# Column sums of an 8192x8192 fp32 matrix: casts and bf16 matmuls replaced by a running sum on VectorE and fp32 matmuls in four column tiles

## The chip, the cores and the metric

The kernel runs on one core of a Trainium2 chip. The metric is the device time of the program in microseconds (us): the median of ten runs before the change, and one further execution taken by the hardware profiler, from which the views below come.

## The reference

```python
def setup_inputs():
    return {"x": np.random.randn(8192, 8192).astype(np.float32)}

def reference(x):
    return np.sum(x, axis=0)
```

The output is one row of 8192 fp32 sums, one for each column of x. The matrix has 268 MB, all of which must be read once; the output has 32 KB.

## The kernel before

The matrix is cut into 64 blocks of 128 rows. In a block each row lies on a partition of its own, and one load of 4 MiB, issued from SyncE's queue (SP, L46), brings the whole block (`xt`, 128x8192 fp32) into SBUF. `xt` has four buffers, so up to four loads are issued ahead; the load of block i+4 waits until both casting engines are done with block i.

Each block is cast to bf16 (`xb`, three buffers) in four strips of 2048 columns: strips 0 and 2 on ScalarE (ACT, L50), strips 1 and 3 on VectorE (DVE, L52). Then TensorE (PE) sums over the partitions: 16 matmuls per block (L60), each with a single column of 128 ones as the stationary operand and 512 columns of `xb` as the moving one. The result of a matmul is one row of 512 sums. The first eight column groups add into partition 0 of `psum`, the other eight into partition 64, at the group's offset; the accumulation runs over all 64 blocks (`start` at the first, `stop` at the last), so the running sum stays in PSUM until the end.

After the last block VectorE copies partition 0 of `psum` to SBUF (`res`, L69), ScalarE copies partition 64 (L70), and SP stores the two halves (L71, L72).

The order of the work is that of the program on each engine; the Tile framework puts in the waits between engines and for free buffers. No order is written out by hand.

Of the kernel before, what the change touches and what calls it, by code (L numbers as in the profile page):

```python
# [1 line left out]

# [4 lines left out]


@with_exitstack  # L10
def kernel(
    ctx: ExitStack,
    tc: tile.TileContext,
    x: bass.AP,
    out: bass.AP,
):
    nc = tc.nc
    P = nc.NUM_PARTITIONS
    R, C = x.shape
    assert R % P == 0  # L20
    n_row_blocks = R // P

    N = 512
    assert C % N == 0
    n_col_groups = C // N
    HALF = C // 2

    xr = x.rearrange("(b p) c -> b p c", p=P)

    const_pool = ctx.enter_context(tc.tile_pool(name="const", bufs=1))  # L30
    load_pool = ctx.enter_context(tc.tile_pool(name="loads", bufs=4))
    bf_pool = ctx.enter_context(tc.tile_pool(name="bf", bufs=3))
    psum_pool = ctx.enter_context(tc.tile_pool(name="psum", bufs=1, space=bass.MemoryType.PSUM))
    out_pool = ctx.enter_context(tc.tile_pool(name="out", bufs=1))

    ones = const_pool.tile([P, 1], mybir.dt.bfloat16)
    nc.gpsimd.memset(ones, 1.0)  # L37

    psum = psum_pool.tile([P, HALF], mybir.dt.float32)

    nsplit = 4
    CS = C // nsplit
    for i in range(n_row_blocks):
        xt = load_pool.tile([P, C], mybir.dt.float32)
        xb = bf_pool.tile([P, C], mybir.dt.bfloat16)
        nc.sync.dma_start(out=xt, in_=xr[i])  # L46
        for s in range(nsplit):
            eng = nc.scalar if s % 2 == 0 else nc.vector
            if eng is nc.scalar:
                eng.copy(out=xb[:, s * CS:(s + 1) * CS], in_=xt[:, s * CS:(s + 1) * CS])  # L50
            else:
                eng.tensor_copy(out=xb[:, s * CS:(s + 1) * CS], in_=xt[:, s * CS:(s + 1) * CS])  # L52
        for g in range(n_col_groups):
            if g < n_col_groups // 2:
                opart = 0
                off = g * N
            else:
                opart = 64
                off = (g - n_col_groups // 2) * N
            nc.tensor.matmul(  # L60
                out=psum[opart : opart + 1, off : off + N],
                lhsT=ones,
                rhs=xb[:, g * N : (g + 1) * N],
                start=(i == 0),
                stop=(i == n_row_blocks - 1),
            )

    res = out_pool.tile([P, HALF], mybir.dt.float32)
    nc.vector.tensor_copy(out=res[0:1, :], in_=psum[0:1, :])  # L69
    nc.scalar.copy(out=res[64:65, :], in_=psum[64:65, :])  # L70
    nc.sync.dma_start(out=out[0:HALF], in_=res[0:1, :])  # L71
    nc.sync.dma_start(out=out[HALF:C], in_=res[64:65, :])  # L72


# [1 line left out]
_INS = ['x']  # L76
_OUTS = [((8192,), 'float32')]


# [23 lines left out]
```

## Time and profile before

| | us |
|---|---|
| median of 10 runs | 646.08 |
| lowest to highest | 645.23 to 646.59 |
| profiled execution, its own time | 645.64 |
| span of the profiled execution, first to last instruction | 643.8 |
| TensorE matmuls busy (1024) | 337.7 |
| ScalarE busy (130) | 241.6 |
| VectorE busy (129) | 155.6 |
| mean DMA rate over the span | 417 GB/s |

The mean granted clock of TensorE was 0.707 of full speed. How the profile is read: the page's first part gives busy time per engine, with the number of instructions; its second part cuts the span into 40 slices and gives the busy share of each in tenths. The chain of waits follows the work that ended last back from the end: a line has its start, its length and what the time went to, either an instruction or the wait for a load. The timeline lists instructions with start, length, engine, line (L50 is line 50 of the kernel), operation, output and input, and in brackets how long the engine had been idle and what ended that. A group of instructions shows, after its shapes and count, the total busy time in us and the mean of one in ns, and then the idle time ahead of it. A busy TensorE is not TensorE at its peak: its matmuls are pipelined and their ends are modelled.

### The profile page before, as it was taken

What the parts mean: (1) busy time and instruction counts of PE and PEld (TensorE: products, weight loads), DVE (VectorE), ACT (ScalarE), POOL (GpSimd) and SP (SyncE); (2) the same over time, 40 slices, a digit from 0 to 9 for tenths busy, and PEclk for the clock granted to TensorE, in tenths of its full rate; (3) what the DMA queues carried; (4) which work ended last, traced back from release to release, by engine and by line L of the source; (5) the groups of instructions that cost most, each with busy time, mean ns of one, the idle gap of its engine ahead of it and who ended that gap; (6) DMA issues with size and microseconds to landing.
All of it is one profiled execution on the core that took longest, in us unless ns stands there. A gap on an engine that the chain in (4) does not pass through costs nothing.

```text
span 643.8 us, 2724 instructions
## 1 busy us (share of the span) xinstructions
PE 337.7 (52%) x1024; PEld 97.6 (15%) x1024; DVE 155.6 (24%) x129; ACT 241.6 (38%) x130; POOL 0.3 (0%) x5
## 2 busy tenths in 40 slices
PE   1464654645645644655546546645556447446542
PEld 0111111111111111111111111111111111111110
DVE  1122122221221221221221221221221222222213
ACT  2244242442442442442442432433433433423423
POOL 0000000000000000000000000000000000000000
PEclk9767668667677687677666766687677776776676
DMA  9999999999999999999999999999999999999980
GB/s 385 430 423 436 441 423 425 438 440 424 422 442 432 429 423 446 425 432 422 444 428 432 426 439 428 434 425 440 429 432 427 434 436 427 430 436 436 425 347 2
DMA packets 9233, 268.64 MB, mean 417 GB/s; under 512 B 1026, under 2 KB 1026, under 8 KB 1026
## 3 DMA queue, kind: packets, MB, share of 16 engines
q1 hardware_dynamic: 9220, 268.47, 97.0%
q8 instruction: 8, 0.13, 0.1%
q14 instruction: 5, 0.04, 0.0%
HBM read 268.44 MB, written 0.03 MB: 417 GB/s over the span
## 4 chain that ended last, share of the span: by engine, by line
DMA 88%; ACT 5%; issue 4%; DVE 1%; PE 1%; SPq 0%; ACTq 0%
DMA xt<-in_x_dram 88%; ACT xb L50 5%; DVE res L69 1%; PE psum L60 1%; ACT res L70 1%; SPq L46 0%; ACTq L50 0%
## 5 line engine op out<-in xcount | busy, mean ns | idle before, releaser
L60 PE MATMUL psum<-xb,ones 128*1 128x512 bf16 x1024 | 337.7, 572 | 295.4 <-DVE xb L52 289.5
L50 ACT CAST xb<-xt 128x2048 bf16<-128x2048 f32 x128 | 236.7, 1896 | 391.9 <-DMA xt<-in_x_dram 391.9
L52 DVE CAST xb<-xt 128x2048 bf16<-128x2048 f32 x128 | 151.2, 1224 | 478.1 <-DMA xt<-in_x_dram 478.1
L60 PEld LDWEIGHTS <-ones 128*1 128x1 bf16 x1024 | 97.6, 107 | 535.0 <-issue 522.2
L70 ACT COPY res<-psum 1x4096 f32<-1x4096 f32 x1 | 3.6, 3562 | 7.0 <-DVE res L69 7.0
L69 DVE COPY res<-psum 1x4096 f32<-1x4096 f32 x1 | 4.4, 4410 | 3.9 <-PE psum L60 3.9
L50 ACT ACT_TABLE_LOAD x1 | 1.3, 1283 | 0.7 <-PEq L87 0.7
L37 POOL MEMSET ones<- 128x1 bf16 x1 | 0.1, 102 | 0.3 <-POOLq L87 0.3
L87 POOL MEMSET const-bfloat16-1.0<- 128x1 bf16 x1 | 0.1, 101 | 0.0
L87 POOL MEMSET const-uint8-127<- 128x1 uint8 x1 | 0.1, 101 | 0.0
L87 POOL MEMSET const-float32-0.0<- 128x1 f32 x1 | 0.1, 98 | 0.2 <-issue 0.2
L87 POOL MEMSET const-float32-1.0<- 128x1 f32 x1 | 0.1, 98 | 0.0
## 6 DMA issues: line engine op xcount, KB each, us to landing
xt<-in_x_dram SPq DMA_DIRECT2D x64, 4096.0 KB, 35.0
out_dram<-res SPq DMA_DIRECT2D x2, 16.0 KB
```

Source lines behind the costliest of these rows:

```text
L37: nc.gpsimd.memset(ones, 1.0)
L50: eng.copy(out=xb[:, s * CS:(s + 1) * CS], in_=xt[:, s * CS:(s + 1) * CS])
L52: eng.tensor_copy(out=xb[:, s * CS:(s + 1) * CS], in_=xt[:, s * CS:(s + 1) * CS])
L60: nc.tensor.matmul(out=psum[opart : opart + 1, off : off + N], lhsT=ones, rhs=xb[:, g * N : (g + 1) * N], start=(i == 0), stop=(i == n_row ...
L69: nc.vector.tensor_copy(out=res[0:1, :], in_=psum[0:1, :])
L70: nc.scalar.copy(out=res[64:65, :], in_=psum[64:65, :])
L87: nc = _bacc.Bacc("TRN2", target_bir_lowering=False, num_devices=1)
```

## The change

- A load now brings two adjacent rows of x to each partition: 32 blocks of 256 rows, 8 MiB each (`xt`, 128 partitions x 2 rows x 8192 columns, 64 KB on each partition), in three buffers instead of four. There is no cast and no bf16 tile.
- For tiles 0 to 29 VectorE carries a running sum. In each tile it adds the running sum of the tile before (that tile's second row) to the first row, in place, and then the first row to the second row, in place; the second row is the running sum from there on. In tile 0 there is only the second of these adds.
- TensorE works only at the end. The stationary operand is 128x32 fp32 ones. The 8192 columns are cut into six pieces of 2048, 2048, 2048, 1024, 512 and 512 columns; each piece is cut into four parts, and part j is summed into the partitions 32j to 32j+31 of the piece's own PSUM tile (one of the four column tiles of the array). First come all pieces of tile 29's running sum, then both rows of tile 30 (`near`), then, piece by piece, both rows of tile 31 (`last`).
- Tile 30 is one load. Tile 31 is loaded in five strips of 4096, 2048, 1024, 512 and 512 columns, all from SP's queue.
- As soon as a piece has its last matmul, VectorE copies its PSUM tile to SBUF and four rows of it (partitions 0, 32, 64, 96) are stored: from SP's queue, for the last piece from ScalarE's.

```diff
+STRIPS = [
+    [(2048, 4), (2048, 4)],
+    [(2048, 4)],
+    [(1024, 4)],
+    [(512, 4)],
+    [(512, 4)],
+]
...
-    xr = x.rearrange("(b p) c -> b p c", p=P)
+    xr = x.rearrange("(b p k) c -> b p k c", p=P, k=K)
...
-    load_pool = ctx.enter_context(tc.tile_pool(name="loads", bufs=4))
-    bf_pool = ctx.enter_context(tc.tile_pool(name="bf", bufs=3))
...
+    load_pool = ctx.enter_context(tc.tile_pool(name="loads", bufs=3))
...
-    ones = const_pool.tile([P, 1], mybir.dt.bfloat16)
+    ones = const_pool.tile([P, 32], F32)
...
+    def column_sums(src, piece, start, stop):
+        _, c0, w, nj, n, ps, _ = piece
+        for j in range(nj):
             nc.tensor.matmul(
-                out=psum[opart : opart + 1, off : off + N],
+                out=ps[32 * j : 32 * j + 32, :],
                 lhsT=ones,
-                rhs=xb[:, g * N : (g + 1) * N],
-                start=(i == 0),
-                stop=(i == n_row_blocks - 1),
+                rhs=src[:, c0 + j * n : c0 + (j + 1) * n],
+                start=start,
+                stop=stop,
+                skip_group_check=True,
             )
...
+    prev = None
+    for t in range(n_blocks - 2):
+        xt = load_pool.tile([P, K, C], F32, tag="xt")
+        nc.sync.dma_start(out=xt, in_=xr[t])
+        a, b = xt[:, 0], xt[:, 1]
+        if prev is not None:
+            nc.vector.tensor_tensor(out=a, in0=a, in1=prev[:, 1], op=ADD)
+        nc.vector.tensor_tensor(out=b, in0=b, in1=a, op=ADD)
+        prev = xt
+
+    near = load_pool.tile([P, K, C], F32, tag="xt")
+    nc.sync.dma_start(out=near, in_=xr[n_blocks - 2])
+    last = load_pool.tile([P, K, C], F32, tag="xt")
+    t = n_blocks - 1
+    c = 0
+    for strip in STRIPS:
+        w = sum(w for w, _ in strip)
+        nc.sync.dma_start(out=last[:, :, c : c + w], in_=xr[t][:, :, c : c + w])
+        c += w
+
+    for piece in pieces:
+        column_sums(prev[:, 1], piece, True, False)
+    for piece in pieces:
+        for k in range(K):
+            column_sums(near[:, k], piece, False, False)
+    for piece in pieces:
+        s, c0, w, nj, n, ps, res = piece
+        for k in range(K):
+            column_sums(last[:, k], piece, False, k == K - 1)
+        rows = 32 * nj
+        nc.vector.tensor_copy(out=res[0:rows, :], in_=ps[0:rows, :])
+        eng = nc.scalar if s == len(STRIPS) - 1 else nc.sync
+        eng.dma_start(
+            out=out[c0 : c0 + w].rearrange("(j i) -> j i", j=nj),
+            in_=res[0 : 32 * (nj - 1) + 1 : 32, :],
+        )
```

More of the change, by code (lines that the diff above doesn't have):

```diff
@@ L7 @@
 from concourse._compat import with_exitstack
+F32 = mybir.dt.float32
+ADD = mybir.AluOpType.add
+STRIPS = [
[5 more added lines that the diff above has]
+]
 @with_exitstack
@@ L19 @@
     R, C = x.shape
[L20 to L26, printed above, removed]
-    xr = x.rearrange("(b p) c -> b p c", p=P)
-    const_pool = ctx.enter_context(tc.tile_pool(name="const", bufs=1))
-    load_pool = ctx.enter_context(tc.tile_pool(name="loads", bufs=4))
-    bf_pool = ctx.enter_context(tc.tile_pool(name="bf", bufs=3))
-    psum_pool = ctx.enter_context(tc.tile_pool(name="psum", bufs=1, space=bass.MemoryType.PSUM))
@@ L34 @@
-    out_pool = ctx.enter_context(tc.tile_pool(name="out", bufs=1))
-    ones = const_pool.tile([P, 1], mybir.dt.bfloat16)
-    nc.gpsimd.memset(ones, 1.0)
[L39 to L59, printed above, removed]
+    K = 2
@@ new lines @@
+    assert R % (P * K) == 0
+    assert sum(w for s in STRIPS for w, _ in s) == C
+    n_blocks = R // (P * K)
+    xr = x.rearrange("(b p k) c -> b p k c", p=P, k=K)
+    const_pool = ctx.enter_context(tc.tile_pool(name="const", bufs=1))
+    load_pool = ctx.enter_context(tc.tile_pool(name="loads", bufs=3))
+    psum_pool = ctx.enter_context(
+        tc.tile_pool(name="psum", bufs=1, space=bass.MemoryType.PSUM)
+    )
+    ones = const_pool.tile([P, 32], F32)
+    nc.gpsimd.memset(ones, 1.0)
@@ L60 @@
+    pieces = []
+    c0 = 0
+    for s, strip in enumerate(STRIPS):
+        for w, nj in strip:
+            n = w // nj
+            i = len(pieces)
+            ps = psum_pool.tile([P, n], F32, name=f"ps{i}", tag=f"ps{i}")
+            res = const_pool.tile([P, n], F32, name=f"res{i}", tag=f"res{i}")
+            pieces.append((s, c0, w, nj, n, ps, res))
+            c0 += w
+    def column_sums(src, piece, start, stop):
+        _, c0, w, nj, n, ps, _ = piece
+        for j in range(nj):
             nc.tensor.matmul(
-                out=psum[opart : opart + 1, off : off + N],
+                out=ps[32 * j : 32 * j + 32, :],
@@ L62 @@
                 lhsT=ones,
-                rhs=xb[:, g * N : (g + 1) * N],
-                start=(i == 0),
-                stop=(i == n_row_blocks - 1),
-            )
[L68 to L72, printed above, removed]
+                rhs=src[:, c0 + j * n : c0 + (j + 1) * n],
@@ new lines @@
+    nc.sync.dma_start(out=near, in_=xr[n_blocks - 2])
[21 more added lines that the diff above has]
+            in_=res[0 : 32 * (nj - 1) + 1 : 32, :],
+        )
```

## The prediction

> **What bounds the kernel now.** I read the page first: the span, the slices, the queue that carries the loads.
>
> ```profile
> span 643.8 us, 2724 instructions
> PE 337.7 (52%) x1024; PEld 97.6 (15%) x1024; DVE 155.6 (24%) x129; ACT 241.6 (38%) x130; POOL 0.3 (0%) x5
> DMA  9999999999999999999999999999999999999980
> q1 hardware_dynamic: 9220, 268.47, 97.0%
> ```
>
> No engine is busy for more than 52% of the span, while the load queue is busy for 97% of it. The DMA slices are full from the first to the 38th and drop only in the last two. So the span is a load stream with a short head and a tail that does no loading. The chain of waits gives the period of the stream and the pieces of the tail.
>
> ```profile
> 2.12 39.97 DMA xt<-in_x_dram
> ...
> 45.91 36.57 DMA xt<-in_x_dram
> ...
> 86.30 35.04 DMA xt<-in_x_dram
> ...
> 125.17 35.02 DMA xt<-in_x_dram
> ...
> 588.14 1.74 issue
> ...
> 591.80 35.01 DMA xt<-in_x_dram
> 626.90 1.91 ACT xb L50
> 628.85 4.32 PE psum L60 x15
> 633.20 4.42 DVE res L69
> 637.65 3.56 ACT res L70
> ```
>
> Each link of the chain is four loads deep, one turn of the four buffers. From 86.30 to 125.17 are 38.87 us, so one 4 MiB load takes 9.72 us, or about 432 GB/s (4.194 MB / 9.72 us). The tail begins where the last load has landed, at 626.90, and lasts 643.8 − 626.90 = 16.9 us: casts, matmuls, a copy on VectorE, a copy on ScalarE that waits for VectorE, a store. Nothing of it lies beside loading. The timeline gives the same landings directly, through the casts that wait for them, and the last store.
>
> ```profile
> 0.73 35.72 SPq L46 DMA_DIRECT2D xt<-in_x_dram  x7
> 12.97 3.70 ACT L50 CAST xb<-xt 128x2048 bf16<-128x2048 f32 x2 [10.96 <-DMA xt<-in_x_dram]
> 588.08 3.70 ACT L50 CAST xb<-xt 128x2048 bf16<-128x2048 f32 x2 [6.02 <-DMA xt<-in_x_dram]
> 607.50 3.70 ACT L50 CAST xb<-xt 128x2048 bf16<-128x2048 f32 x2 [6.01 <-DMA xt<-in_x_dram]
> 626.90 3.70 ACT L50 CAST xb<-xt 128x2048 bf16<-128x2048 f32 x2 [6.00 <-DMA xt<-in_x_dram]
> 641.23 0.25 SPq L72 DMA_DIRECT2D out_dram<-res  x1
> ```
>
> The profiled execution took 645.64 us, 1.84 us more than its span, and lies 0.07% under the median of 646.08. I work on its trace and add the 1.84 us at the end.
>
> **The stream.** The same 268 MB are loaded in the same order, in 8 MiB loads: one per two of the old. At 2 × 9.72 = 19.4 us each, tile 31 (the last) lands at 626.9, tile 30 at 607.5 and tile 29 at 588.1, the rows above. The first load is issued at 0.73 and lands at 12.97, so 12.24 − 9.72 = 2.5 us are lead-in, unchanged. Removing the casts takes nothing from this; they run beside the stream.
>
> Two things could move the stream. Half as many loads could lose less between loads, and the second link (45.91 to 86.30, 40.4 us) lost 1.5 us at the start that may not recur: a gain of at most about 2 us. The last tile comes as strips of 4096, 2048, 1024, 512 and 512 columns, so its rows arrive in shorter runs (2 KB in the end). If the two 512-column strips, 1 MiB or 2.4 us together, ran at half rate, that is 2.4 us more; no row shows it. I take +0.5 us, nearer to the full rate that all the loads show, which puts the last landing at 627.4.
>
> **VectorE's sum.** This is new and must fit beside the stream. Each of 30 tiles gets two fp32 adds of 128x8192 (the first tile one). The trace has no two-input operation; the nearest rows are these.
>
> ```profile
> L52 DVE CAST xb<-xt 128x2048 bf16<-128x2048 f32 x128 | 151.2, 1224 | 478.1 <-DMA xt<-in_x_dram 478.1
> L69 DVE COPY res<-psum 1x4096 f32<-1x4096 f32 x1 | 4.4, 4410 | 3.9 <-PE psum L60 3.9
> L60 PEld LDWEIGHTS <-ones 128*1 128x1 bf16 x1024 | 97.6, 107 | 535.0 <-issue 522.2
> ```
>
> By the cast an add takes 4 × 1.22 = 4.9 us, by the PSUM copy 2 × 4.41 = 8.8 us. An add reads two streams, so I take the slower row: 8.7 us, as its fixed part (some 0.14 us) comes once for 8192 columns, not twice. Two adds are 17.4 us against 19.4 us per tile: hidden, with a slack of 2 us per tile, and VectorE is never behind when a tile lands. The cover is gone when an add exceeds 9.7 us.
>
> The loads wait for VectorE now: tile t's buffer is free when the first add of tile t+1 has read its second row, 8.7 us after that tile landed. In the three-buffer rotation load t+2 is then still running for another 19.4 − 8.7 = 10.7 us, and the lead-in is 2.5 us, so SP's queue has the next load waiting in time. Behind a waiting load on SP stand only later loads and, at the very end, the stores. The strips of tile 31 wait for the first add of tile 29 (588.1 + 8.7 = 596.8), before tile 30 has landed.
>
> **TensorE at the end.** This decides the case. TensorE does nothing until tile 29's sum is complete at 588.1 + 17.4 = 605.5. Then it must take in one row per partition of that sum, two of tile 30 and two of tile 31: in units of one 128x512 fp32 matmul 16 + 32 + 32 = 80, in order. Call the price of one unit, after whatever the four column tiles gain by running side by side, p. The trace has only bf16 matmuls; these two windows cover one burst of 16, at half clock and then near full.
>
> ```profile
> 618.50:621.50 3.00, 2.93 (x9) 0.97 (x10) 1.10 (x1) 2.41 (x2) 0.00 (x0) 0.50 0.96 415
> 621.50:623.20 1.70, 1.70 (x10) 0.42 (x6) 0.00 (x0) 0.00 (x0) 0.00 (x0) 0.94 1.07 463
> ```
>
> The columns are length, busy time by engine, granted clock, DMA share, GB/s. In time at full clock the burst is 3.00 × 0.50 + 1.70 × 0.94 = 3.1 us for 16 matmuls, 0.19 us each; the first 3 us of a burst cost double, 1.5 us once.
>
> The ends for p: 0.05 us if an fp32 matmul costs a bf16 one's time and all four tiles gain fully (0.19 / 4), and 0.76 us if it costs double for its double bytes, double again because the clock stays at the 0.50 of the first window, and the tiles gain nothing (0.19 × 2 × 2). I take 0.19 us, the row as it stands: two effects of unknown size pull on it from opposite sides. [...]
>
> With p = 0.19: tile 29's sum takes 605.5 to 610.0, tile 30 until 616.1. Tile 31's strips land at about 617.2, 622.1, 624.5, 625.7 and 627.4 and need 16, 8, 4, 2 and 2 units, each done before the next lands: TensorE is idle when the last strip comes. What follows 627.4 is two units (0.4), VectorE's copy of 128 columns out of PSUM (4410 − 4096 / 0.96 = 143 ns fixed and 133 ns of columns: 0.3) and the store, 643.8 − 641.23 = 2.6 us from issue to the end as now, plus 0.1 us of handing on: 3.4 us. ScalarE's queue, which issues this store, holds nothing else. The other copies and stores fall while later strips are loading.
>
> Sum: 643.8 − 16.9 + 0.5 + 3.4 = 630.8 us of span, 632.6 us with the 1.84. Against 645.64 that is a gain of 13 us, 2.0%, all of it the tail.
>
> When p grows, the backlog does not matter up to 0.26 us, as TensorE still waits for the last strip. Beyond, TensorE runs without a pause from 605.5: the time is 605.5 + 1.5 + 80p + 2.95 (copy, store and handing on) + 1.84 = 611.8 + 80p. Ten nanoseconds of p are 0.8 us of the kernel, and the old time of 646.1 is reached at p = 0.43 us.
>
> **Rivals.** First: the column tiles run one after the other (which is also the case that the change does not do what it says, four tiles at once). With p = 0.76 the time is 611.8 + 60.8 = 672.6 us, 4% slower; the point from which this decides is p = 0.43 us. For it: in the trace matmuls follow one another strictly, and no two outputs in neighbouring column tiles are ever in work together, so no gain is shown. Against it: the four outputs of a group lie on separate partitions and depend on nothing of each other, and a price between these ends is enough.
>
> Second: the tiles overlap, but each matmul shows its weight load. That load takes 107 ns in the row of VectorE's fence, so p = 0.19 + 0.11 = 0.30 us, and the time 611.8 + 24 = 635.8 us; with a larger fp32 load or a weaker gain, up to p = 0.42 and 645 us. For it: 120 matmuls (6 pieces, 4 tiles, 5 rows) each load 32 columns of fp32 instead of one of bf16. Against it: in the two windows 16 loads (0.97 + 0.42 us busy) lie inside time in which TensorE is busy throughout (2.93 of 3.00, 1.70 of 1.70), so today they cost nothing. [...]
>
> Third: VectorE becomes the bound. Tile 0 lands 31 × 19.4 before 626.9, at about 25. At an add of 10.5 us, 59 adds end at 25 + 59 × 10.5 = 644.5, and all 80 units, the copy and the store follow: 1.5 + 15.2 + 2.95 + 1.84, together 666 us. It decides from 9.7 us. For it: an add reads two streams and writes one in place while the DMA fills the same memory; against it: no row of VectorE is slower than 1.08 ns per column (4410 / 4096), and 8192 of those are 8.8 us.
>
> Fourth: the stream gains its 2 us and the strips cost nothing: about 630 us.
>
> **How the numbers follow.** About 0.2% (1.3 us) is what a measurement of this kernel can tell from no change. The forecast (p up to 0.26, stream as now or slightly better) has 0.64, the fourth case 0.04 of its own, the second, between 635 and 645 us, 0.14; the first from p = 0.44 up has 0.11, VectorE or a slower stream 0.04. About 0.03 is left for a p close to 0.43, where the tail merely changes its owner. So faster 0.82, within 0.2% 0.03, slower 0.15. The predicted time is 632.6 us. The range is 629.5 to 645: the lower end is the stream's gain, the upper the end of the second case; what it leaves out is the slow side above it and little below.
>
> **What would show it.** VectorE's adds at 8.7 us each, with idle time in front of the first of each pair ended by the load; a DMA row of nines to the end; load landings 19.4 us apart; TensorE's first matmul at about 605 and idle waits for the strips of tile 31; the chain ending in a DMA wait, a short copy and a store on ScalarE's queue within 4 us of the last landing. TensorE busy without a pause from 605 until after the last landing would show p above 0.26, and its length divided by 80 gives p. VectorE busy without idle time and loads waiting for it would show the third rival. The prediction is wrong if the last landing is not within 2 or 3 us of 627, or if more than 5 us lie behind it.

## The result and the profile after

The median fell from 646.10 us (28 runs, 645.23 to 646.93) to 629.21 us (8 runs, 628.74 to 629.34). The ratio is 0.974, with a 95% interval of 0.973 to 0.975. The profiled execution took 629.19 us, with a span of 627.3 us. The forecast was 632.6 us and its range began at 629.5 us: the change gained 16.9 us where 13 were expected, and the time lies just below the range.

The page, for the lines shown of before:

```profile
span 627.3 us, 698 instructions
PE 20.9 (3%) x240; PEld 7.7 (1%) x240; DVE 515.9 (82%) x65; POOL 0.3 (0%) x5
DMA  9999999999999999999999999999999999999996
q1 hardware_dynamic: 5864, 268.47, 99.0%
```

The load queue is busy for 99% of the span in place of 97%, and its last slice is at 6 tenths in place of 0: the tail without loading has nearly gone. VectorE went from 24% to 82%. The packets fell from 9220 to 5864, because a run of 64 KB is one packet (of the kernel with more small matmuls, below, 1310 packets over 512 B bring 85.85 MB between 102 and 300 us, 65.5 KB each) where two of 32 KB were two.

The groups of instructions by line, for VectorE's new adds:

```profile
L81 DVE TENSOR_TENSOR xt<-xt 128x8192 f32<-128x8192 f32 x29 | 252.1, 8693 | 65.0 <-DMA xt<-in_x_dram 65.0
L82 DVE TENSOR_TENSOR xt<-xt 128x8192 f32<-128x8192 f32 x30 | 260.7, 8692 | 23.5 <-DMA xt<-in_x_dram 22.5
```

An add takes 8.69 us, and VectorE's idle time is ended by loads: it waits for the stream, not the stream for it.

The timeline, from the first landings to the end (the adds and the first matmuls of a strip start when the load has landed):

```profile
22.50 8.69 DVE L82 TENSOR_TENSOR xt<-xt 128x8192 f32<-128x8192 f32 x1 [22.50 <-DMA xt<-in_x_dram]
...
564.58 8.69 DVE L81 TENSOR_TENSOR xt<-xt 128x8192 f32<-128x8192 f32 x1 [1.88 <-DMA xt<-in_x_dram]
...
583.89 8.69 DVE L81 TENSOR_TENSOR xt<-xt 128x8192 f32<-128x8192 f32 x1 [1.90 <-DMA xt<-in_x_dram]
...
601.41 6.26 PE L64 MATMUL ps<-xt,ones 128*32 128x512 f32 x48 [601.41 <-DVE xt L82]
...
607.48 7.07 PE L64 MATMUL ps<-near,ones 128*32 128x512 f32 x96
...
618.71 1.92 PE L64 MATMUL ps<-last,ones 128*32 128x512 f32 x16 [0.72 <-DMA last<-in_x_dram]
...
623.69 0.64 PE L64 MATMUL ps<-last,ones 128*32 128x128 f32 x16 [0.63 <-DMA last<-in_x_dram]
624.40 0.29 DVE L106 COPY res<-ps 128x128 f32<-128x128 f32 x1 [0.98 <-PE ps L64]
624.73 1.08 ACTq L108 DMA_DIRECT2D out_dram<-res  x1
```

The last strip lands at 623.69, and 3.6 us follow (627.3 − 623.69): 0.7 of matmuls, 0.3 of copy, 2.6 of store. TensorE idles in front of the strips (0.72, 0.63 us), so it is not what the end waits for. The 32 units of tile 30 took 7.07 us, 0.22 us each; a fp32 matmul appears as two instructions (240 in all for 120 matmuls).

The difference of the spans, 16.5 us, is therefore 13.3 us of tail (16.9 to 3.6) and 3.2 us of stream (last landing 626.90 to 623.69). Up to tile 29 the stream is even 4.2 us earlier (588.08 to 583.89), of which 1 us is lost again at the end. The forecast had the first part and missed the second; the experiments are mostly about the second.

The 4.2 us can be split from the landings. By distance I mean the median time from one landing to the next: 9.715 us before (19.43 per 8 MiB) and 19.32 after. Before, nearly all loads keep to it within 0.02 us; after, single ones lie between 19.27 and 19.54. A few come later, by 0.4 to 1.5 us, which I call pauses. Of the 4.2 us, 0.18 lie in the first 8 MiB (22.68 to 22.50), 29 × (19.43 − 19.32) = 3.2 in the distance, and 0.8 in the pauses and what else departs from the distance (1.93 us before, 1.11 after: the time from that landing to tile 29's, less 29 times the distance).

### The profile page after: what moved, and what is told of

Read it like the earlier page. It is cut to its first block, busy times and chain, and to the rows that moved or that the text cites. A ratio compares the mean times of both kernels' runs of the same rounds, so it can differ in the third digit from the quotient of the medians.

```text
span 627.3 us, 698 instructions
## 1 busy us (share of the span) xinstructions
PE 20.9 (3%) x240; PEld 7.7 (1%) x240; DVE 515.9 (82%) x65; POOL 0.3 (0%) x5
## 3 DMA queue, kind: packets, MB, share of 16 engines
q1 hardware_dynamic: 5864, 268.47, 99.0%
## 4 chain that ended last, share of the span: by engine, by line
DMA 78%; DVE 21%; SPq 0%; issue 0%; PE 0%; DVEq 0%
DMA xt<-in_x_dram 73%; DVE xt L81 21%; DMA last<-in_x_dram 5%; SPq L93 0%; PE ps L64 0%; SPq L78 0%; DVEq L81 0%; DVE res L106 0%
## 5 line engine op out<-in xcount | busy, mean ns | idle before, releaser
L81 DVE TENSOR_TENSOR xt<-xt 128x8192 f32<-128x8192 f32 x29 | 252.1, 8693 | 65.0 <-DMA xt<-in_x_dram 65.0
L82 DVE TENSOR_TENSOR xt<-xt 128x8192 f32<-128x8192 f32 x30 | 260.7, 8692 | 23.5 <-DMA xt<-in_x_dram 22.5
L64 PE MATMUL ps<-xt,ones 128*32 128x512 f32 (+2 forms) x48 | 6.3, 692 | 601.4 <-DVE xt L82 601.4
L106 DVE COPY res<-ps 128x512 f32<-128x512 f32 (+2 forms) x6 | 3.1, 514 | 20.3 <-PE ps L64 20.3
L64 PEld LDWEIGHTS ps<-xt,ones 128*32 128x32 f32 x48 | 2.1, 148 | 605.3 <-issue 605.2
L64 PE MATMUL ps<-last,ones 128*32 128x512 f32 (+2 forms) x96 | 7.9, 454 | 2.1 <-DMA last<-in_x_dram 2.1
L64 PE MATMUL ps<-near,ones 128*32 128x512 f32 (+2 forms) x96 | 7.1, 450 | 0.0
L64 PEld LDWEIGHTS ps<-near,ones 128*32 128x32 f32 x96 | 3.0, 110 | 3.9 <-issue 3.5
L64 PEld LDWEIGHTS ps<-last,ones 128*32 128x32 f32 x96 | 2.6, 109 | 7.2 <-DMA last<-in_x_dram 4.6
```

Source lines behind the costliest of these rows:

```text
L64: nc.tensor.matmul(out=ps[32 * j : 32 * j + 32, :], lhsT=ones, rhs=src[:, c0 + j * n : c0 + (j + 1) * n], start=start, stop=stop, skip_gro ...
L81: nc.vector.tensor_tensor(out=a, in0=a, in1=prev[:, 1], op=ADD)
L82: nc.vector.tensor_tensor(out=b, in0=b, in1=a, op=ADD)
L106: nc.vector.tensor_copy(out=res[0:rows, :], in_=ps[0:rows, :])
```

## The experiments

### Number of loads, length of runs, or the casts

A run is a stretch of adjacent bytes that goes to one partition. Three theories for the distance of the loads. R: each run costs a DMA engine a fixed time, and adjacent rows halve the runs. L: each load costs a fixed time, and there are half as many. C: the casts and matmuls slowed the stream.

**Rows apart.**

```diff
-    xr = x.rearrange("(b p k) c -> b p k c", p=P, k=K)
+    xr = x.rearrange("(b k p) c -> b p k c", p=P, k=K)
```

> Loads of 8 MiB as in the changed kernel, but each partition gets rows p and p+128 of its block, so a load consists of 256 runs of 32 KB in place of 128 runs of 64 KB. The number of loads (31 whole ones) stays. Theory R (a fixed cost per run, 12 ns on each DMA engine, worked out from 19.43 against 19.33 us per 8 MiB): the period goes back to 19.43 us, tile 29 lands 3 us later and the time is about 632.3 us. Theory L (a fixed cost per load, 0.1 us): unchanged, 629.2 us. Theory C (the casts and the matmuls of the old kernel slowed the stream by their SBUF traffic): unchanged, 629.2 us.

Measured: 629.57 us (629.47 to 629.84). The distance is 19.35 us. R's 3 us did not come; 0.4 us did, and the old kernel's median differs by 0.6 us between the sets of runs in which these experiments were timed (645.57 to 646.17). By the landings, tile 29 came at 584.48 in place of 583.89.

**One row per load.**

```diff
-        nc.sync.dma_start(out=xt, in_=xr[t])
+        for k in range(K):
+            nc.sync.dma_start(out=xt[:, k], in_=xr[t][:, k])
... (tile 30 the same way)
```

> The changed kernel with each whole tile loaded by two loads of 4 MiB, one row per partition each: 64 loads of 32 KB runs as in the old kernel, with the new arithmetic. Theory R: 632.3 us. Theory L: 632.3 us. Theory C: unchanged, 629.2 us, as no cast is there.

Measured: 629.77 us (629.51 to 629.95), distance 9.68 us per 4 MiB. Against L: twice the loads, with 32 KB runs, cost 0.6 us in all and not 3.

**Half the partitions per load.**

```diff
-        nc.sync.dma_start(out=xt, in_=xr[t])
+        for h in range(2):
+            nc.sync.dma_start(out=xt[64 * h : 64 * h + 64], in_=xr[t][64 * h : 64 * h + 64])
... (tile 30 the same way)
```

> The changed kernel with each whole tile loaded by two loads of 4 MiB, one for each half of the partitions: twice the loads, but runs of 64 KB. Theory R: unchanged, 629.2 us. Theory L: 632.3 us. Theory C: 629.2 us. If the two halves use the DMA engines less evenly than a whole tile does, it is slower than all of these.

Measured: 1285.64 us (1283.79 to 1288.34), twice the time. The page's queue line and two landings in the timeline of this kernel:

```profile
q1 hardware_dynamic: 6360, 268.47, 99.7%
```

```profile
610.71 8.69 DVE L82 TENSOR_TENSOR xt<-xt 128x8192 f32<-128x8192 f32 x1 [23.05 <-DMA xt<-in_x_dram]
...
651.18 8.69 DVE L82 TENSOR_TENSOR xt<-xt 128x8192 f32<-128x8192 f32 x1 [23.05 <-DMA xt<-in_x_dram]
```

The DMA engines are as busy as before (99.7%) and move half as much: 8.39 MB in 40.47 us, 207 GB/s. As a test of L it failed, because it changed something larger. Why loads of 64 partitions run at half the rate isn't shown here.

**The old kernel with two-row loads.**

```diff
+    K = 2
...
-    xr = x.rearrange("(b p) c -> b p c", p=P)
+    xr = x.rearrange("(b p k) c -> b p k c", p=P, k=K)
...
-    load_pool = ctx.enter_context(tc.tile_pool(name="loads", bufs=4))
+    load_pool = ctx.enter_context(tc.tile_pool(name="loads", bufs=2))
...
-        xt = load_pool.tile([P, C], mybir.dt.float32)
+        if i % K == 0:
+            pair = load_pool.tile([P, K, C], mybir.dt.float32)
+            nc.sync.dma_start(out=pair, in_=xr[i // K])
+        xt = pair[:, i % K]
...
-        nc.sync.dma_start(out=xt, in_=xr[i])
```

> The old kernel (casts, bf16 matmuls, its whole tail) with loads of 8 MiB that bring two adjacent rows to each partition, in two buffers: one part of the change alone. Theories R and L: the stream gains what the changed kernel's gained, 3 to 4 us, so 642 to 643 us. Theory C: 646 us as before, because the casts remain.

Measured: 645.77 us (ratio 1.000, 0.999 to 1.001), the number that C gives. But the chain of waits says otherwise:

```profile
593.39 31.27 DMA pair<-in_x_dram
624.77 1.91 ACT xb L53
626.72 6.52 PE psum L63 x30
633.26 4.42 DVE res L72
637.71 3.56 ACT res L73
```

The last load landed at 624.77, 2.1 us earlier than before, with a distance of 19.35 us. The tail got longer by as much, 643.9 − 624.8 = 19.1 us against 16.9, since 8 MiB have to be cast and summed after the last landing. The stream gained and the tail gave it back: the total says nothing of C.

### Instruction loads

In the trace of before, the DMA queues asked for single stretches show what lies in the two larger pauses (61.61 to 72.86, and 480.86 to 490.96, where 9.72 is the rule). These are rows of the windows 61 to 73 and 480 to 491 us; the columns are packets, MB and share of 16 engines:

```profile
q1 hardware_dynamic: 170, 5.01, 97.3%
q8 instruction: 1, 0.02, 0.6%
...
q1 hardware_dynamic: 166, 4.75, 100.9%
q14 instruction: 2, 0.02, 0.4%
```

Both hold packets that bring instructions. Theory I: these packets pass through the same DMA engines, and the stream pauses for some of them. The changed kernel has 698 instructions in place of 2724, and 4 such packets in place of 13.

**No running sum.** TensorE sums all rows; the change without its last step.

```diff
-        if prev is not None:
-            nc.vector.tensor_tensor(out=a, in0=a, in1=prev[:, 1], op=ADD)
-        nc.vector.tensor_tensor(out=b, in0=b, in1=a, op=ADD)
-        prev = xt
+        for piece in pieces:
+            for k in range(K):
+                column_sums(xt[:, k], piece, t == 0 and k == 0, False)
...
-    for piece in pieces:
-        column_sums(prev[:, 1], piece, True, False)
```

> The changed kernel without its last step: VectorE adds nothing, TensorE sums all 64 rows per partition by fp32 matmuls in four column tiles (32 units of 0.22 us, 7.1 us per tile of 19.3 us). Theory I (the engines' instructions come in by DMA too, and each time one of these loads sits on a DMA engine, the stream pauses): some 12,000 instructions on TensorE's queue in place of 480, so more pauses than in the old kernel (2.0 us there): 631 to 635 us. Theory C in its remaining form (TensorE's reading slows the stream): period above 19.35 us. If neither holds: 629 us, the running sum brings nothing.

Measured: 631.49 us (631.33 to 631.63); its page has 6274 instructions, half of what I expected. The distance is 19.30 us, so TensorE's reading slows nothing, but three intervals are 20.74, 20.77 and 20.77 us long. In the timeline, each of them from one landing to the next:

```profile
22.55 9.84 PE L64 MATMUL ps<-xt,ones 128*32 128x512 f32 x96 [22.55 <-DMA xt<-in_x_dram]
43.29 9.70 PE L64 MATMUL ps<-xt,ones 128*32 128x512 f32 x96 [10.90 <-DMA xt<-in_x_dram]
...
236.44 8.71 PE L64 MATMUL ps<-xt,ones 128*32 128x512 f32 x96 [9.48 <-DMA xt<-in_x_dram]
257.21 8.56 PE L64 MATMUL ps<-xt,ones 128*32 128x512 f32 x96 [12.06 <-DMA xt<-in_x_dram]
...
450.35 9.27 PE L64 MATMUL ps<-xt,ones 128*32 128x512 f32 x96 [10.61 <-DMA xt<-in_x_dram]
471.12 9.12 PE L64 MATMUL ps<-xt,ones 128*32 128x512 f32 x96 [11.50 <-DMA xt<-in_x_dram]
```

The instruction queue q8 in five windows of this kernel, the long intervals and the stretches between them: 22.5 to 43.3, 43.3 to 236.4, 236.4 to 257.2, 257.2 to 450.3, 450.3 to 471.2 us:

```profile
q8 instruction: 1, 0.02, 0.3%
...
q8 instruction: 7, 0.11, 0.2%
...
q8 instruction: 1, 0.02, 0.3%
...
q8 instruction: 7, 0.11, 0.2%
...
q8 instruction: 1, 0.02, 0.3%
```

Each long interval has one packet of q8 in it, the calm stretches between them seven each: the first, the ninth and the seventeenth of the kernel's 24 packets cost the stream 1.45 us each, and the others nothing that shows. The old kernel agrees: of its eight q8 packets the first lies in the pause from 61.61 to 72.86, the other seven in intervals of 9.71 to 9.73 us. Why it is one in eight, these views can't say. Three pauses are 4.4 us, where the changed kernel has 1.1 and a microsecond at the end; that accounts for the 2.3 us by which this kernel is slower. So the running sum on VectorE brings fewer instructions, not relief for a busy engine: TensorE needs half of each interval here (8.6 to 9.8 of 19.3 us in the rows above). A packet has 16 KB (24 packets, 0.39 MB on this kernel's page). What the packets cost TensorE, these views don't show.

**More small matmuls.**

```diff
+    spare = psum_pool.tile([P, 32], F32, name="spare", tag="spare")
...
+        for d in range(16):
+            nc.tensor.matmul(out=spare[0:32, :], lhsT=ones,
+                rhs=b[:, 32 * d : 32 * d + 32], start=True, stop=True,
+                skip_group_check=True)
         prev = xt
```

> The changed kernel with 16 more matmuls per tile, 32 columns each, into a PSUM tile that nobody reads, as each tile's sum is complete: about 1,900 more instructions for TensorE, next to no SBUF traffic, nothing on the way to the end. Theory I: pauses in the landings, as in the old kernel, 1 to 2 us in all: 630 to 631 us, with packets of the instruction queues at the pauses. If the pauses came from casts or from full-width matmuls: 629.2 us.

Measured: 629.96 us (629.80 to 630.47), 0.75 us slower, with 11 instruction packets and one new interval of 20.55 us (81.00 to 101.55). As theory I has it, at the lower end: adding instructions alone, with next to no data, brings a pause. The first of the nine q8 packets lies in that interval; the ninth comes in the last 40 us (see "The end").

### The distance again

**Casts on one engine.** Two runs.

```diff
-            eng = nc.scalar if s % 2 == 0 else nc.vector
+            eng = nc.vector
```

> The old kernel with all four casts on VectorE. The tail is 1.2 us longer (4 casts of 1.22 us against two of 1.89). If ScalarE's casts are what made the load period 9.717 us where the changed arithmetic with the same loads has 9.68: period 9.68 us, last landing about 624.5, time about 645 us. If any cast with its bf16 write does it: period 9.717 us, 647.3 us.

> The old kernel with all four casts on ScalarE. The tail is 3.8 us longer (4 casts of 1.89 us against two). If ScalarE's casts lengthen the load period: 9.75 us, last landing about 629, time about 652 us. If VectorE's casts do: 9.68 us, last landing 624.5, time 647.5 us. If any cast does: 9.717 us, 650 us.

Measured: 645.73 us on VectorE (ratio 1.000, 0.999 to 1.001) and 647.38 us on ScalarE (1.003, 1.002 to 1.004). The distance is 9.71 us in both: neither engine's casts are special. Both totals are 1.6 and 2.6 us below what I expected for that case. About 0.4 and 1.7 us of this lie in the tail, which is 17.7 and 19.0 us long: the chain has one cast and then matmuls, so the later casts run beside matmuls, which I had not subtracted.

**Loads alone.**

```diff
+        if i < n_row_blocks - 1:
+            nc.vector.tensor_copy(out=seen[:, i : i + 1], in_=xt[:, 0:1])
+            continue
...
```

> The old kernel's 64 loads in four buffers, with nothing beside them but a copy of one column per tile on VectorE; casts and matmuls are left out for all blocks but the last, so only that block is summed. If the work beside the stream lengthens the period: 9.68 us or less per load, last landing about 622 us or earlier, time 641 us. If the period belongs to the loads themselves (their number, run length or the four buffers): 9.717 us, last landing 626 us, as the instruction loads are gone, 645 us at most.

Measured: 644.38 us (one run). Two landings from the timeline:

```profile
119.91 0.15 DVE L48 COPY seen<-xt 128x1 f32<-128x1 f32 x1 [9.56 <-DMA xt<-in_x_dram]
...
304.49 0.15 DVE L48 COPY seen<-xt 128x1 f32<-128x1 f32 x1 [9.56 <-DMA xt<-in_x_dram]
```

These are 19 loads: 184.58 / 19 = 9.715 us. With nothing beside them the old loads come at the same distance, so theory C falls. The 1.5 us pause is gone, with the packets of queue q8.

**Five buffers**, and **rows apart with casts.**

```diff
-    load_pool = ctx.enter_context(tc.tile_pool(name="loads", bufs=4))
+    load_pool = ctx.enter_context(tc.tile_pool(name="loads", bufs=5))
-    bf_pool = ctx.enter_context(tc.tile_pool(name="bf", bufs=3))
+    bf_pool = ctx.enter_context(tc.tile_pool(name="bf", bufs=1))
```

> The old kernel with five load buffers in place of four (and one bf16 buffer in place of three), so that one more load is queued. If the depth of the queue sets the period: 9.68 us, last landing 624.5, time 643.8 us. If not: 9.717 us and 646 us.

> The old kernel with 32 loads of 8 MiB whose runs are 32 KB (rows p and p+128 on a partition). If the number of loads brought the shorter period beside casts: 19.35 us per load, last landing 624.8, 645.8 us as with adjacent rows. If the run length did: 19.43 us, last landing 627, 648 us.

Measured: 646.14 us with five buffers (ratio 1.000, 0.999 to 1.001; 9.71 us), so one more queued load does nothing; 647.72 us (1.003, 1.002 to 1.004) with rows apart. Landings of the two-row loads beside casts, rows apart and then adjacent:

```profile
276.88 4.63 DVE L55 CAST xb<-pair 128x2048 bf16<-128x2048 f32 x4 [14.80 <-DMA pair<-in_x_dram]
...
529.42 4.63 DVE L55 CAST xb<-pair 128x2048 bf16<-128x2048 f32 x4 [14.80 <-DMA pair<-in_x_dram]
```

```profile
276.35 4.63 DVE L55 CAST xb<-pair 128x2048 bf16<-128x2048 f32 x4 [14.71 <-DMA pair<-in_x_dram]
...
527.88 4.63 DVE L55 CAST xb<-pair 128x2048 bf16<-128x2048 f32 x4 [14.71 <-DMA pair<-in_x_dram]
```

13 loads in 252.54 and 251.53 us: 19.43 and 19.35 us. Same loads, same number, same buffers; only the runs are 32 or 64 KB. Theory R holds here: 128 runs fewer save 0.08 us. If they lie evenly on the 16 DMA engines of the page, that is 8 on each, and 10 ns per run by this estimate.

**Adds on the old loads, and the new loads alone.**

```diff
+        if i > 0:
+            nc.vector.tensor_tensor(out=xt, in0=xt, in1=prev, op=mybir.AluOpType.add)
+        prev = xt
+        if i < n_row_blocks - 1:
+            continue
...
```

> The old kernel's 64 loads in four buffers; in place of the casts VectorE adds the running sum of the block before to each block (8.7 us of each 9.7), and only the last block's sum is cast and goes through the matmuls. A buffer is released 18.4 us after its landing in place of 3.7. If a shorter queue shortens the period: 9.68 us. If four buffers of 4 MiB have 9.715 whatever the release: 9.715 us.

> The same with five load buffers, one load more in the queue. If a shorter queue shortens the period: between 9.68 and 9.715 us, longer than with four. If the adds themselves do it: 9.68 us in both. If neither: 9.715 in both.

> The changed kernel's loads (8 MiB, 64 KB runs, three buffers) with nothing beside them but a copy of one column on VectorE for tiles 0 to 29; those tiles are left out of the sums. A buffer is released at its landing. If a shorter queue shortens the period: 19.35 us as beside casts, longer than the changed kernel's 19.32. If the two-row loads alone set it: 19.32 us.

Measured (one run each): 652.49 us and 652.81 us, 9.715 us per load in both; 630.05 us with 19.35 us per 8 MiB for the new loads alone. So adds as such do not shorten the distance, nor does a late release of four or five buffers.

Taken together: 32 KB runs have 19.43 us per 8 MiB in every kernel with single-row buffers and in the two-buffer one, whatever runs beside them; 64 KB runs have 19.35 beside casts and alone. With the changed kernel's three two-row buffers and its adds, each loses a little more: 19.35 with 32 KB runs, 19.32 with 64 KB; with matmuls in place of the adds it is 19.30. What that last part is (0.08 us with short runs, 0.03 with long ones, less than single loads of the changed kernel differ) stays open. The adds in single-row buffers, the number of loads and a deeper queue of small buffers were tried and are not it; 32 KB runs in three two-row buffers with nothing beside them were not tried.

### The end

**Tile 31 in one load.**

```diff
-    for strip in STRIPS:
-        w = sum(w for w, _ in strip)
-        nc.sync.dma_start(out=last[:, :, c : c + w], in_=xr[t][:, :, c : c + w])
-        c += w
+    nc.sync.dma_start(out=last, in_=xr[t])
```

> The changed kernel with tile 31 as one load in place of five strips. The last landing comes at 583.9 + 2 x 19.33 = 622.6 us, 1.1 us earlier than the last strip, but all 32 units of TensorE follow it: 32 x 0.22 = 7.1 us, then 3.0 us of copy and store. Span 632.6, time 634.5 us: the strips are worth some 5 us. If the strips did not cost the stream that 1.1 us, the landing is at 623.7 and the time 635.6 us.

Measured: 636.86 us (636.49 to 637.28), 7.6 us slower. From the timeline:

```profile
584.08 8.69 DVE L81 TENSOR_TENSOR xt<-xt 128x8192 f32<-128x8192 f32 x1 [1.91 <-DMA xt<-in_x_dram]
...
623.59 8.74 PE L64 MATMUL ps<-last,ones 128*32 128x512 f32 x96 [9.06 <-DMA last<-in_x_dram]
```

The strips are worth 7.6 us, more than I expected: after 9 us of idling the matmuls took 8.74 us in place of 7.07. The landing comes 39.5 us after tile 29's, with strips 39.8. So the strips themselves cost the stream 0.3 us, and most of the microsecond that it loses at the end (two distances are 38.6) is not their price.

That rest goes with an instruction packet. In both kernels the first packet of q8 comes in this stretch, at 612 to 615 us, and wherever the first one comes in the middle of the stream, in the old kernel, its five variants with casts and the two with more matmuls, it lies in a pause. Two kernels with the same strips tell them apart. Without the running sum, the packet that comes at 610.5 is the 23rd, which costs nothing; in the new loads alone the packet at 615.3 is the first. From tile 30's landing to that of the second strip (the last two of these four rows are the new loads alone):

```profile
606.31 9.79 PE L64 MATMUL ps<-near,ones 128*32 128x512 f32 x96 [10.10 <-DMA near<-in_x_dram]
...
620.96 1.92 PE L64 MATMUL ps<-last,ones 128*32 128x512 f32 x16 [1.24 <-DMA last<-in_x_dram]
...
603.59 9.38 PE L64 MATMUL ps<-near,ones 128*32 128x512 f32 x96 [603.59 <-DMA near<-in_x_dram]
...
619.53 1.92 PE L64 MATMUL ps<-last,ones 128*32 128x512 f32 x16 [2.60 <-DMA last<-in_x_dram]
```

It takes 14.65 us with the 23rd packet and 15.94 with the first. From tile 29 to the last strip the kernel without the running sum needs 38.9 us (587.01 to 625.94); the kernel with more small matmuls, whose ninth packet comes at 617.8, needs 40.0. How such a packet holds up the stream is still open.

**Last rows in strips.** Tile 31's first rows whole, its second rows in strips of 4096, 2048, 1024 and 1024.

```diff
-    [(512, 4)],
-    [(512, 4)],
+    [(1024, 4)],
...
+    nc.sync.dma_start(out=last[:, 0], in_=xr[t][:, 0])
     for strip in STRIPS:
-        nc.sync.dma_start(out=last[:, :, c : c + w], in_=xr[t][:, :, c : c + w])
+        nc.sync.dma_start(out=last[:, 1, c : c + w], in_=xr[t][:, 1, c : c + w])
... (matmuls of the first rows ahead of those of the second)
```

> The changed kernel with tile 31's first rows as one load of 4 MiB, its second rows in strips of 4096, 2048, 1024 and 1024 columns: the same bytes in the last strip, 40 runs per DMA engine in place of 80, the shortest 4 KB in place of 2 KB. If the end of the stream (39.8 us from tile 29's landing to the last, against 2 x 19.3) is slow for its short runs: up to 1 us less, 628.2 us. If it is slow for TensorE's instructions coming in at that time: unchanged, 629.2 us.

Measured: 629.61 us (629.05 to 629.68). Short runs are not what costs at the end.

**Last store from SP.**

```diff
-        eng = nc.scalar if s == len(STRIPS) - 1 else nc.sync
+        eng = nc.sync
```

> The changed kernel with the last piece's store issued from SP instead of ScalarE. The issue took 1.08 us on ScalarE's queue, 0.25 us on SP's in the old kernel's last store. If that length is on the way to the end: 0.8 us less, 628.4 us. If only the landing counts, or SP is still busy with the store before: unchanged, 629.2 us.

Measured: 629.04 us (628.68 to 629.26), no difference that the runs can tell. The 1.08 us on ScalarE's queue are not on the way to the end.

**Tile after tile.** The first rival's point.

```diff
... (column_sums with a fifth argument takes only that column tile; tile 29 is queued the same way)
-    for piece in pieces:
-        for k in range(K):
-            column_sums(near[:, k], piece, False, False)
+    for j in range(4):
+        for piece in pieces:
+            for k in range(K):
+                column_sums(near[:, k], piece, False, False, j)
```

> The changed kernel with the matmuls of tiles 29 and 30 in another order: all pieces of column tile 0 first, then all of tile 1, 2 and 3, so that a matmul's neighbours in TensorE's queue work in its own column tile. Same matmuls, same data. If the price of 0.22 us per unit is the gain of four tiles side by side (the first rival's point): each unit costs four times as much, 0.88 us, the 48 units end at 601.4 + 2.7 + 48 x 0.88 = 646.3, tile 31's 32 units 7.1 us later, then 3.0 us of copy and store: span 656.5, time 658.4 us. If a fp32 unit costs 0.22 us in any order: unchanged, 629.2 us.

Measured: 653.73 us (ratio 1.013, 1.011 to 1.014), slower than the old kernel. Tile 30 in the timeline:

```profile
615.74 25.73 PE L64 MATMUL ps<-near,ones 128*32 128x512 f32 x92
```

The same 32 units take 25.7 us in place of 7.07, 0.80 us each. Queued tile after tile the matmuls run one by one, one weight load every 0.43 us; queued in turns, four run side by side, four weight loads every 0.43 us, a gain of 3.6. The order of the matmuls alone decides whether the change gains or loses.

None of these kernels is measurably faster than the changed one.

## Why the prediction was wrong

The sum was 643.8 − 16.9 + 0.5 + 3.4 + 1.84 = 632.6 us; measured is 629.2.

- *The stream, +0.5 us, with "a gain of at most about 2 us"*: this step failed. Measured is −3.2 us to the last landing, 3.7 us from the forecast. The prediction's own sign for this, a last landing within 2 or 3 us of 627, failed with 623.7. I took 9.72 us per 4 MiB for a property of the bytes. It is in part one of the runs (19.43 us per 8 MiB with 32 KB runs against 19.35 with 64 KB, 2.3 us in 29 tiles), which I did not price at all: I asked what half as many loads would save, which turned out to be nearly nothing, and not what half as many runs would. Another 0.03 us per tile, 0.9 us, comes with the new arrangement and stays unexplained. This split holds for the old arrangement; given 32 KB runs again, the changed kernel lost only 0.6 us by tile 29, so most of the shorter distance would have come without the longer runs, by something that no run here singles out. The pause in the second link of the chain, which I saw and put at 1.5 us, goes with the first packet of q8. It is not saved but moved: in the changed kernel that packet comes at 612 us and holds up the end of the stream. Up to tile 29, 0.8 us of pauses went in all.
- *The strips at half rate, up to 2.4 us*: the mechanism was wrong. One load lands 0.3 us earlier, so that is what the strips cost; the rest of the microsecond lost at the end is there without strips and goes with the instruction packet.
- *VectorE, 8.7 us per add*: right, 8.69. The slower of the two rows was the one to take.
- *Loads that wait for VectorE*: right; the stream never ran dry.
- *TensorE, p = 0.19 us*: 0.22 us measured, near the forecast in part by luck: a unit alone costs 0.80 us, about four times the bf16 row that I took, and the four tiles gain 3.6. I had no size for either from the traces and let them cancel. The slow start was longer: tile 29's 16 units took 6.1 us in place of 4.5. Both were hidden, as said, because p stayed under 0.26.
- *3.4 us after the last landing*: right, 3.6. The 0.96 columns per ns by which its copy was priced stood in no row of before; the runs show them: the copies of 512 and of 128 columns take 692 and 292 ns, 384 columns in 400 ns, and the last one took 0.29 us.
- *First rival*: its point is real. One by one a unit costs 0.80 us (forecast 0.76), and with tiles 29 and 30 queued so the time is 653.7 us. The program's order avoids it.
- *Second rival*: no. The weight loads of a group of four (0.13 us) fit into the 0.43 us that its matmuls take: tile 30 needs 16 such groups (32 units, two instructions each, four at a time) and took 7.07 us.
- *Fourth case, "about 630 us"*: this is where the result fell, with 0.04 of the chance. Its 2 us were the one pause and a little for fewer loads; the length of the runs had no part in them.

## What to carry to other kernels

In a kernel that is bound by its loads, the tail without loading is the large and safe gain: narrow the last loads so that only a little work follows the last one, and check that the engines keep up by one price per unit. Where the stream is at its ceiling, count the runs and the instructions as well as the bytes: beside the casts, runs of 64 KB gave 0.3% over 32 KB, and the kernel with a ninth of the instructions was 0.4% faster than the one without a running sum. The matmuls in column tiles ran side by side only where the tiles took turns in the queue: 0.22 us a unit, against 0.80 tile after tile.

## What the runs showed of the hardware

- Instructions came in by packets on DMA queues of their own, q8 and q14 (8 and 5 packets in the old kernel, 2 and 2 in the changed one). In the kernel with 24 packets of 16 KB on q8, the first, ninth and seventeenth held up the stream by 1.45 us each (20.77 against 19.30 us), the others not; in the old kernel the first of eight did (11.25 against 9.715 us).
- A load of 64 partitions ran at 207 GB/s, half of what 128 partitions had (8.39 MB in 19.32 us, 434 GB/s).
- TensorE's slow start is not in the recorded clock. In the changed kernel the clock reads 1.00 in both of these windows (the columns as in the prediction), yet the weight loads come every 0.85 us in the first and every 0.43 us in the second:

```profile
601.40:607.48 6.08, 6.07 (x48) 2.12 (x52) 0.00 (x0) 0.00 (x0) 1.00 0.94 402
607.48:614.30 6.82, 6.82 (x104) 2.94 (x100) 0.00 (x0) 0.00 (x0) 1.00 0.99 418
```

```profile
603.09 0.22 PEld L64 LDWEIGHTS ps<-xt,ones 128*32 128x32 f32 x4 [0.63 <-issue]
603.95 0.22 PEld L64 LDWEIGHTS ps<-xt,ones 128*32 128x32 f32 x4 [0.63 <-issue]
...
608.34 0.13 PEld L64 LDWEIGHTS ps<-near,ones 128*32 128x32 f32 x4 [0.29 <-issue]
608.77 0.13 PEld L64 LDWEIGHTS ps<-near,ones 128*32 128x32 f32 x4 [0.30 <-issue]
```

- A cost of fewer bytes in flight did not show. The changed kernel issues a load when 0.55 of the load in progress is left (tile 30's at 573.30, where tile 29 lands at 583.89), so it has half a load to one and a half of 8 MiB outstanding, 4 to 12 MiB. The old kernel, whose buffers come free 3.7 us after a landing, has 2.6 to 3.6 loads of 4 MiB, 10 to 14 MiB, and its stream was slower (19.43 us per 8 MiB against 19.32).
